# A Griffin-style decoder layer on one core: the first 256 tokens of the gated head outputs are turned to channels by transposing transfers through device memory

## The chip, the cores and the metric

The kernel runs on one core of one Trainium2 chip. The time is device microseconds (us) of that core from launch to end; three runs of the kernel before gave a median of 817.22 us (816.57 to 817.22). The profile is one further execution of the same program.

Engines are named as in the profile: PE is TensorE's matmuls and PEld its weight loads, DVE is VectorE, ACT is ScalarE, POOL is GpSimd, SP is SyncE. "SPq" and "POOLq" are transfers issued by those two. Each engine runs its own instructions in the order in which they stand; engines wait for each other by semaphores.

## The reference

One layer on x of 512 tokens by 1024 channels, in float32. The part that the change touches is branch B, gated linear attention with four heads of 256 output channels:

```python
u = _rmsnorm(h, norm1_g[l])
proj = u @ w_in[l]
a_glu, q, k, v, r, g_low, gate_a, gate_b = _split_cols(proj)
...
o = _gla_chunked(qh, kh, vh, gkh)
o = o * lax.rsqrt(jnp.mean(o * o, axis=-1, keepdims=True) + EPS) * gla_norm_g[l].astype(jnp.float32)
o = o.reshape(bsz, seq, GLA_VDIM).astype(x.dtype) * jax.nn.silu(r)
y_gla = o @ w_gla_out[l]

merged = jax.nn.sigmoid(gate_a) * y_conv + jax.nn.sigmoid(gate_b) * y_gla
h = h + merged @ w_o[l]
```

Behind it stand a second RMSNorm, an up-projection to 2 x 2816 channels with a short convolution, a gated down-projection and a last RMSNorm.

## The kernel before, in words

**Products.** Every float32 operand of a large product is split into a high part `hi` (type float32r, made by an ACT copy) and a low part `lo` (the rest, made by a DVE subtraction), and a product is three matmuls, low by high, high by low and high by high (`mm3`, L537, whose matmuls stand on L541 to L543). Weights come from device memory into four `raw` buffers of 128x1024 words, are split into `whi` (L426, L456) and `wlo` (L427, L464), and are used by TensorE. `weight` (L482) keeps the split weights two steps ahead of their use, and `refill` keeps SP's loads a few tiles ahead of that. The loads stand in SP's order as the list `order` has them (L244 to L274).

**The r-gate.** The projection of r (`seven("w_r", ...)`, L573) is a product of 2x2 blocks in seven steps, a11, a12, s1, n2, s4, n3 and a22. It gives r with tokens on the partitions, in tiles `rt[t, n]` of 128 tokens by 512 channels (t = 0 to 3, n = 0 or 1). `put_r` (L1544) takes each finished tile out of PSUM, applies silu, and multiplies the head outputs `ot[t, n]` by it on DVE (L1561, L1565). The tiles are finished in this order: (0,0) and (1,0) by step a12, (0,1) and (1,1) by s4, (2,1) and (3,1) by n3, (2,0) and (3,0) by a22.

**Turning to channels.** The projection `w_gla` needs the gated outputs with channels on the partitions. `gated_o` (L1246) does that for one 128-channel tile m: four TensorE transposes of 128x128 (one for each 128 tokens) into a PSUM bank `ax` (L1250), an ACT activation that scales by the norm's gain into `hi` (L1257), and a DVE operation that leaves `lo` (L1258). m = 0 to 3 come from n = 0, m = 4 to 7 from n = 1. The eight tiles are called in four pairs: 4 and 5 by `r_at` (L1568) at the end of the r projection, then 6 and 7, 0 and 1, 2 and 3 behind the steps x1, x3 and x2 of the next unit (L1592).

**The unit that follows.** `two_tiles` (L1344) makes two output tiles of a gate projection together, again in seven half-wide steps, in four parts named x1, x3, x2 and x4 after their weights. The first such unit is for `w_gb`, tiles 6 and 7. Its weights are the two loaded tiles (x1, x2) and sums of them made by POOL in `two_sums` (L395, additions on L398). In part x3 ACT copies the accumulators out of PSUM (`put`, L1350, the copy on L1351), and part x2 goes on accumulating in the same banks. Then come `w_gla` 0 and 1, which read all eight turned tiles (`tile_of`, L1444), and the next units.

**Order.** A scheduler in the recording layer orders each engine's instructions. `tc.issue_after(x)` lets what is recorded inside it come only behind the instruction x on its engine. Tiles come from pools with a fixed number of buffers per tag; the tag `btmp` has two, of which one holds the square sums' operand until L1060 and L1061 have read it.

## Time and profile before

| What | Value |
|---|---|
| median of 3 runs | 817.22 us (816.57 to 817.22) |
| the profiled execution, its own time | 816.96 us |
| its span, first to last instruction | 815.3 us |
| granted TensorE clock | 0.998 |
| PE busy in the span | 807.5 us (99%) |
| DVE, ACT, POOL busy | 86%, 60%, 24% |
| TensorE transposes of L1250 | 32, the first at 284.2 us, the last at 296.2 us |

A row of the timeline gives the start in us from the span's start, the duration in us, the engine, the line, the operation, the tile written and those read, the shape, how many such instructions follow one another, and in brackets how long the engine had been idle and what ended it. Durations of matmuls overlap, since they are pipelined: the distance between two starts is what one costs. A row of the DMA issues gives the tile and tensor, the issuing queue, the count, the size of one and the median time from its issue to its landing.

### The profile page before, as it was taken

How to read it: one execution, taken by the hardware profiler on the slowest of the kernel's cores; microseconds unless marked ns; L12 is line 12 of the kernel's file. 1: busy time of each engine (PE TensorE's matmuls, PEld its weight loads, DVE VectorE, ACT ScalarE, POOL GpSimd, SP SyncE). 2: the span in 40 equal slices, each digit the busy share in tenths (PEclk: the TensorE clock that was granted, in tenths of full speed). 3: DMA queues.
4: the chain of work that ended last, by engine and by line, in shares of the span. 5: the costliest groups of instructions: out<-in, count | busy, mean ns of one | idle time of the engine just before them, and what ended most of it. 6: DMA issues, size and time to landing. Idle time of an engine off the chain costs nothing.

```text
span 815.3 us, 11441 instructions
## 1 busy us (share of the span) xinstructions
PE 807.5 (99%) x4215; PEld 693.2 (85%) x4215; DVE 700.7 (86%) x1108; ACT 487.9 (60%) x746; POOL 192.5 (24%) x166
## 2 busy tenths in 40 slices
PE   9999999999999999999999999999999999999996
PEld 7888888788888898989888898898889988899885
DVE  6679999998998988486779899979976999789896
ACT  6667788677546575494435655556435663466655
POOL 2025433332204332122001100320133300522010
PEclk9999999999999999999999999999999999999999
DMA  8487858745831232432458613145732345334662
GB/s 337 146 198 179 187 160 176 161 119 135 186 95 60 78 130 78 137 105 95 164 124 220 190 57 126 52 154 156 144 127 92 142 117 167 105 104 171 165 129 105
DMA packets 36616, 113.60 MB, mean 139 GB/s; under 512 B 3704, under 2 KB 8960, under 8 KB 36560
## 3 DMA queue, kind: packets, MB, share of 16 engines
q1 hardware_dynamic: 29200, 86.92, 30.8%
q0 software_dynamic: 7200, 25.69, 18.0%
q8 instruction: 33, 0.54, 0.3%
q14 instruction: 23, 0.19, 0.1%
q10 hardware_dynamic: 160, 0.27, 0.1%
HBM read 110.76 MB, written 2.10 MB: 138 GB/s over the span
## 4 chain that ended last, share of the span: by engine, by line
PE 84%; DVE 13%; issue 1%; ACT 1%; DMA 1%; SPq 0%; DVEq 0%; ACTq 0%
PE mm L541 20%; PE mm L542 20%; PE mm L543 20%; DVE c L902 5%; PE cv L541 4%; PE cv L542 4%; PE cv L543 4%; DVE aside L902 3%; PE ax L542 2%; PE ax L541 2%; PE ax L543 2%; PE ax L1230 1%; PE ax L1232 1%; DMA kept<-in_w_r_dram 1%; PE ax L1212 0%
## 5 line engine op out<-in xcount | busy, mean ns | idle before, releaser
L541 PE MATMUL mm<-uh,wlo 128*128 128x512 f32 (+1 forms) x532 | 193.9, 364 | 0.2 <-DVE wlo L464 0.2
L542 PE MATMUL mm<-ul,whi 128*128 128x512 f32 (+1 forms) x532 | 191.6, 360 | 0.0
L543 PE MATMUL mm<-uh,whi 128*128 128x512 f32 (+1 forms) x532 | 191.4, 360 | 0.0
L427 DVE TENSOR_TENSOR wlo<-raw,whi 128x1024 fp32r<-128x1024 f32 x82 | 96.0, 1178 | 36.0 <-ACT whi L426 32.2
L398 POOL TENSOR_TENSOR raw<-raw,raw 128x512 f32<-128x512 f32 x39 | 63.9, 1638 | 236.3 <-DVE wlo L427 130.9
L541 PEld LDWEIGHTS mm<-uh,wlo 128*128 128x128 f32 x532 | 100.5, 189 | 15.6 <-DVE wlo L464 0.6
L543 PEld LDWEIGHTS mm<-uh,whi 128*128 128x128 f32 x532 | 100.4, 189 | 15.4
L542 PEld LDWEIGHTS mm<-ul,whi 128*128 128x128 f32 x532 | 100.5, 189 | 14.7
L426 ACT CAST whi<-raw 128x1024 fp32r<-128x1024 f32 x82 | 78.9, 965 | 41.4 <-PE mm L543 24.4
L456 ACT CAST whi<-raw 128x1024 fp32r<-128x1024 f32 x80 | 83.5, 1048 | 27.5 <-PE mm L543 13.9
L464 DVE TENSOR_TENSOR wlo<-raw,whi 128x1024 fp32r<-128x1024 f32 x50 | 66.3, 1331 | 7.1 <-ACT whi L456 6.8
L426 ACT CAST whi<-kept 128x1024 fp32r<-128x1024 f32 (+1 forms) x40 | 40.1, 1008 | 32.4 <-DVE kept L374 16.5
L902 DVE SCALAR_TENSOR_TENSOR aside<-cv,pp,aside 128x255 f32<-128x255 f32 (+6 forms) x112 | 52.2, 466 | 0.0
L902 DVE SCALAR_TENSOR_TENSOR c<-aside,btmp,c 128x247 f32<-128x247 f32 (+13 forms) x93 | 52.1, 565 | 0.0
L427 DVE TENSOR_TENSOR wlo<-kept,whi 128x1024 fp32r<-128x1024 f32 (+1 forms) x40 | 47.5, 1191 | 4.9 <-ACT whi L426 4.7
L902 DVE SCALAR_TENSOR_TENSOR c<-cv,pp,c 128x247 f32<-128x247 f32 (+13 forms) x93 | 43.2, 465 | 1.4 <-ACT c L898 1.4
L458 ACT ACTIVATE wlo<-raw 128x1024 fp32r<-128x1024 f32 x28 | 29.4, 1059 | 19.1 <-PE mm L541 19.1
L1351 ACT COPY tmp<-mm 128x256 f32<-128x256 f32 x38 | 14.1, 370 | 35.1 <-PE mm L543 34.3
L1733 DVE SCALAR_TENSOR_TENSOR tmp<-mm,pp,tmp 128x511 f32<-128x511 f32 (+1 forms) x42 | 31.2, 743 | 3.5 <-ACT tmp L1730 3.4
L1733 DVE SCALAR_TENSOR_TENSOR tmp<-tmp,pp,tmp 128x511 f32<-128x511 f32 (+1 forms) x32 | 27.8, 888 | 0.3
L1504 DVE TENSOR_TENSOR hres<-hres,mm 128x512 f32<-128x512 f32 (+1 forms) x37 | 24.7, 676 | 2.2 <-PE mm L543 2.1
L542 PE MATMUL cv<-ul,whi 128*128 128x512 f32 (+1 forms) x72 | 25.6, 356 | 0.0
(514 smaller groups left out, 2078.3 us busy)
## 6 DMA issues: line engine op xcount, KB each, us to landing
raw<-in_w_up_dram SPq DMA_DIRECT2D x44, 512.0 KB, 3.2
raw<-in_w_glu_dram SPq DMA_DIRECT2D x16, 512.0 KB, 5.1
raw<-in_w_down_dram SPq DMA_DIRECT2D x16, 512.0 KB, 3.4
wlo<-in_w_glu_dram POOLq DMA_DIRECT2D x12, 512.0 KB, 7.1
kept<-in_w_down_dram POOLq DMA_DIRECT2D x9, 512.0 KB, 5.5
raw<-in_w_v_dram SPq DMA_DIRECT2D x8, 512.0 KB, 6.0
raw<-in_w_qk_dram SPq DMA_DIRECT2D x8, 512.0 KB, 6.3
raw<-in_w_gb_dram SPq DMA_DIRECT2D x8, 512.0 KB, 4.0
```

What stands on the lines that cost most here:

```text
L398: work = nc.gpsimd.tensor_tensor(out, x, y, ALU.add)
L426: nc.scalar.copy(hi, raw)
L427: two_low[:] = [nc.vector.tensor_tensor(lo, raw, hi.bitcast(F32), ALU.subtract)]
L456: nc.scalar.copy(hi, raw)
L458: pace[0] = nc.scalar.mul(lo, raw, -1.0)
L464: pace[0] = nc.vector.tensor_tensor(lo, raw, hi.bitcast(F32), ALU.subtract)
L541: nc.tensor.matmul(acc, ll, rh, start=first, stop=False, **kw)
L542: nc.tensor.matmul(acc, lh, rl, start=False, stop=False, **kw)
L543: nc.tensor.matmul(acc, lh, rh, start=False, stop=last, **kw)
L902: nc.vector.scalar_tensor_tensor(out[:, j:], x[:, : half_t - j], w, out[:, j:], ALU.mult, ALU.add)
L1504: done = nc.vector.tensor_tensor(hres[t, n][:, c], hres[t, n][:, c], acc[:, c], op)
L1733: nc.vector.scalar_tensor_tensor(z[:, s:], acc[:, : T - s], w[j], z[:, s:], ALU.mult, ALU.add)
```

## The change

For the first 256 tokens (t = 0 and 1) the turn from tokens to channels leaves TensorE. When `ot[t, n]` is gated (`gate_o`), an ACT copy takes its float32 values apart into their lower and upper 16 bit words, in a tile `planes` of 128 x 2 x 512 words in the tag `btmp`. A transfer issued by POOL writes the tile into a new device memory tensor `words`, one for each n, so that its rows are token and word and its columns channels. When both t are there, `turn_o` issues from SP four transfers with `transpose=True`, each of 512 rows by 128 columns of 16 bit words. One lands as 128 channels by 256 tokens, where the two words of a value lie side by side again. So there are four copies, four writes of 256 KB and eight transposing transfers of 128 KB.

`gated_two` replaces `gated_o`, for two tiles m at once: eight TensorE transposes instead of sixteen, into one bank instead of two, for the tokens from 256 on. `half_o` scales and splits the halves apart, in operations of 256 columns instead of 512: from `turned` for the first half, from PSUM for the second. The first halves of m = 4 to 7 (n = 1) are done behind those of m = 0 to 3. The `hi` copies of the `w_gb` weights that come next are put behind the last `planes` copy on ACT.

```diff
@@ split_weight, the weights in pairs and sevens
-                nc.scalar.copy(hi, raw)
+                with tc.issue_after(behind_planes[0].ins) if behind_planes and spec[0] == "w_gb" else ExitStack():
+                    nc.scalar.copy(hi, raw)
...
-    def gated_o(m, bank):
+    last_silu = []
+    turned, words_of = {}, [dram.tile([T, DV * 2], U16, name=nm("words")) for _ in range(2)]
+
+    def words(t, n):
+
+        planes = tp.tile([P, 2, T], U16, tag="btmp", name=nm("planes"), bufs=2)
+        behind_planes[:] = [nc.scalar.copy(planes, ot[t, n].bitcast(U16).rearrange("p (c two) -> p two c", two=2))]
+        rows = words_of[n][2 * t * P : 2 * (t + 1) * P, :]
+        nc.gpsimd.dma_start(rows.rearrange("(p two) c -> p two c", two=2), planes)
+
+    def turn_o(n):
+        if n == 0:
+            four = rp_.tile([P, 4, H], F32, tag="rx", name=nm("turned"), bufs=1)
+            landing = [four[:, j, :] for j in range(4)]
+        else:
+            twos = [rp_.tile([P, 2, H], F32, tag="r", name=nm("turned"), bufs=6) for _ in range(2)]
+            landing = [two[:, j, :] for two in twos for j in range(2)]
+        for j in range(4):
+            nc.sync.dma_start(landing[j].bitcast(U16), words_of[n][:, j * P : (j + 1) * P], transpose=True)
+            turned[4 * n + j] = landing[j]
+
+    def gated_two(m, bank):
         po = bank()
-        c = (m % 4) * P
-        for p in range(NT):
-            nc.tensor.transpose(po[:, p * P : (p + 1) * P], ot[p, m // 4][:, c : c + P], ident)
-        gain = pp[:, PP_GG + m % 2 : PP_GG + m % 2 + 1]
+        for j in range(2):
+            c = (m % 4 + j) * P
+            for p in (2, 3):
+                at = j * H + (p - 2) * P
+                nc.tensor.transpose(po[:, at : at + P], ot[p, m // 4][:, c : c + P], ident)
+        for j in range(2):
+            start_o(m + j)
+            if m < 4:
+                half_o(m + j, slice(0, H), turned[m + j], last_silu)
+            half_o(m + j, slice(H, T), po[:, j * H : (j + 1) * H], last_silu)
+        if m < 4:
+            for j in range(2):
+                half_o(m + 4 + j, slice(0, H), turned[m + 4 + j], low_at)
...
-        nc.scalar.activation(hi, po, AF.Copy, scale=gain)
-        low_at[:] = [nc.vector.scalar_tensor_tensor(lo, po, gain, hi.bitcast(F32), ALU.mult, ALU.subtract)]
-        oa[m] = hi, lo
+        oa[m] = (both[:, 0, :], both[:, 1, :]) if m < 4 else (heap(F32R), heap(F32R))
+
+    def half_o(m, c, x, behind_op):
+        (hi, lo), gain = oa[m], pp[:, PP_GG + m % 2 : PP_GG + m % 2 + 1]
+        with tc.issue_after(behind_op[0].ins):
+            nc.scalar.activation(hi[:, c], x, AF.Copy, scale=gain)
+            low = nc.vector.scalar_tensor_tensor(lo[:, c], x, gain, hi[:, c].bitcast(F32), ALU.mult, ALU.subtract)
+        if m < 4:
+            low_at[:] = [low]
...
+    def gate_o(t, n):
+        nc.vector.tensor_tensor(ot[t, n], ot[t, n], rt[t, n], ALU.mult)
+        if t < 2:
+            words(t, n)
+        if t == 1:
+            turn_o(n)
...
         if (step, t, n) == ("a22", 3, 0):
-            i, j = gated.pop()
-            nc.vector.tensor_tensor(ot[i, j], ot[i, j], rt[i, j], ALU.mult)
+            gate_o(*gated.pop())
+            gated_two(4, ax_bank)
```

Three places of the built order follow; the rows have line, operation, tile written, tiles read and shape, with the buffer's number in the name.

ACT, from the last weights of the r projection (`kept`) to the first activation of the turned tiles, before. `whi_452`, `whi_455`, `whi_470` and `whi_479` are the w_gb unit's weights for x1, x3, x2 and x4:

```order
L426 CAST whi_450_2649<-kept_349_2138 128x1024
L1555 ACTIVATE r_441_2599<-r_441_2599 128x512
L1555 ACTIVATE r_432_2545<-r_432_2545 128x512
L426 CAST whi_452_2683<-raw_448_2644 128x1024
L426 CAST whi_455_2691<-raw_454_2687 128x1024
L1555 ACTIVATE r_433_2559<-r_433_2559 128x512
L1550 ACTIVATE r_457_2708<-cv_403_2412 128x512
```

The same place on ACT in the changed kernel, where `whi_461` is the weight for x1:

```order
L1255 COPY planes_449_2631<-h_254_1608 128x1024
L429 CAST whi_456_2667<-kept_351_2142 128x1024
L1602 ACTIVATE r_444_2606<-r_444_2606 128x512
L1255 COPY planes_451_2654<-h_345_2129 128x1024
L1602 ACTIVATE r_435_2552<-r_435_2552 128x512
L1602 ACTIVATE r_436_2566<-r_436_2566 128x512
L1255 COPY planes_458_2686<-h_346_2131 128x1024
L429 CAST whi_461_2710<-raw_454_2662 128x1024
L429 CAST whi_464_2718<-raw_463_2714 128x1024
L429 CAST whi_478_2772<-raw_455_2663 128x1024
L1597 ACTIVATE r_466_2735<-cv_405_2416 128x512
```

The last three of the four `planes` copies stand in these rows, all ahead of the unit's first weight; the silu of the last gate (`r_466`) moved behind the weights for x3 and x2.

POOL, the additions for the w_gb unit (`raw_454` is the sum tile) and for the next unit, before:

```order
L398 TENSOR_TENSOR raw_454_2687<-raw_448_2644,raw_449_2645 128x512
L398 TENSOR_TENSOR raw_454_2687<-raw_454_2687,raw_449_2645 128x512
L398 TENSOR_TENSOR raw_449_2645<-raw_449_2645 128x512
L398 TENSOR_TENSOR raw_454_2687<-raw_454_2687,raw_448_2644 128x512
L398 TENSOR_TENSOR raw_501_2929<-raw_488_2852,raw_489_2853 128x512
```

The same place on POOL in the changed kernel, where the sum tile is `raw_463`:

```order
L1257 DMA words_197_1285<-planes_430_2521 128x1024
L400 TENSOR_TENSOR raw_463_2714<-raw_454_2662,raw_455_2663 128x512
L400 TENSOR_TENSOR raw_463_2714<-raw_463_2714,raw_455_2663 128x512
L400 TENSOR_TENSOR raw_455_2663<-raw_455_2663 128x512
L1257 DMA words_197_1285<-planes_449_2631 128x1024
L1257 DMA words_198_1286<-planes_451_2654 128x1024
L1257 DMA words_198_1286<-planes_458_2686 128x1024
L400 TENSOR_TENSOR raw_463_2714<-raw_463_2714,raw_454_2662 128x512
```

One write stands ahead of the additions, and three between the third and the fourth of them.

SP, its loads from the w_gb unit's weights on, before:

```order
L292 DMA raw_448_2644<-in_w_gb_dram 128x1024
L292 DMA raw_449_2645<-in_w_gb_dram 128x1024
L296 DMA raw_472_2754<-in_w_gla_dram 128x1024
L296 DMA raw_481_2804<-in_w_gla_dram 128x1024
L292 DMA raw_488_2852<-in_w_ga_dram 128x1024
L292 DMA raw_489_2853<-in_w_ga_dram 128x1024
```

The same place on SP in the changed kernel:

```order
L294 DMA raw_454_2662<-in_w_gb_dram 128x1024
L294 DMA raw_455_2663<-in_w_gb_dram 128x1024
L298 DMA raw_480_2776<-in_w_gla_dram 128x1024
L1267 DMA_TRANSPOSE turned_450_2634<-words_197_1285 128x512 x4
L1267 DMA_TRANSPOSE turned_459_2689<-words_198_1286 128x512 x2
L1267 DMA_TRANSPOSE turned_460_2690<-words_198_1286 128x512 x2
L298 DMA raw_488_2821<-in_w_gla_dram 128x1024
L294 DMA raw_494_2872<-in_w_ga_dram 128x1024
```

All eight transposing transfers stand between the loads of `w_gla` 0 and `w_gla` 1.

More of the change, by code (lines that the diff above doesn't have):

```diff
@@ L1549, in put_r @@
             rt[t, n] = rp_.tile([P, T], F32, tag="r", name=nm("r"), bufs=6)
-            nc.scalar.activation(rt[t, n], acc, AF.Silu)
+            last_silu[:] = [nc.scalar.activation(rt[t, n], acc, AF.Silu)]
         else:
@@ L1592, in pair_7 @@
             if n == 0 and j < 3:
-                for m in ((6, 7), (0, 1), (2, 3))[j]:
-                    gated_o(m, ax_bank)
+                gated_two((6, 0, 2)[j], ax_bank)
                 if j == 2:
```

15 lines of the change are left out of this document (6 added, 9 removed).

## The prediction

> **What bounds the kernel now.** I read the page's busy times and chain first, then a table by stage around the changed work, then the timelines of each engine there.
>
> ```profile
> PE 807.5 (99%) x4215; PEld 693.2 (85%) x4215; DVE 700.7 (86%) x1108; ACT 487.9 (60%) x746; POOL 192.5 (24%) x166
> PE 84%; DVE 13%; issue 1%; ACT 1%; DMA 1%; SPq 0%; DVEq 0%; ACTq 0%
> core 0: us, PE busy (x) PEld busy (x) DVE busy (x) ACT busy (x) POOL busy (x), PEclk, DMA share, GB/s
> 250.00:284.00 34.00, 33.88 (x150) 27.76 (x149) 31.93 (x30) 21.74 (x28) 11.02 (x7) 1.00 0.18 62
> 284.00:300.00 16.00, 16.00 (x129) 15.49 (x128) 13.29 (x18) 12.73 (x21) 3.44 (x3) 1.00 0.41 133
> ```
>
> TensorE is busy for 99% of the span, and in the 16 us in which the turned tiles are made it never stops, at a full granted clock. So each instruction taken off TensorE there is time won, each wait put in front of it is time lost, and nothing later has room to give either back. DMA has room (busy 0.41), ACT and DVE have 3.3 and 2.7 us of it.
>
> **What is removed.** The PE timeline, with the four pairs of turned tiles:
>
> ```profile
> 284.17 1.03 PE L1250 MATMUL ax<-ident,h 128*128 128x128 f32 x8
> 284.96 0.36 PE L541 MATMUL mm<-uh,wlo 128*128 128x256 f32 x1
> ...
> 287.92 1.04 PE L1250 MATMUL ax<-ident,h 128*128 128x128 f32 x8
> 288.71 0.36 PE L541 MATMUL mm<-hq,wlo 128*128 128x256 f32 x1
> ...
> 291.66 1.04 PE L1250 MATMUL ax<-ident,h 128*128 128x128 f32 x8
> 292.45 0.36 PE L541 MATMUL mm<-sumsq,wlo 128*128 128x256 f32 x1
> ...
> 297.70 0.40 PE L541 MATMUL mm<-oa,wlo 128*128 128x512 f32 x1
> 297.93 0.40 PE L542 MATMUL mm<-oa,whi 128*128 128x512 f32 x1
> ```
>
> Eight transposes cost 284.96 - 284.17 = 0.79 us, 0.099 each. The change drops four of every eight, four times: 4 x 0.395 = 1.58 us. That is the whole gain on the path. It is 0.19% of 817.22, and about 0.2% is what a measurement of this kernel can tell from no change, so even the full gain would just fail to show.
>
> **What is added, off the path if all goes well.** ACT did eight activations of 512 columns and now does sixteen of 256, DVE likewise:
>
> ```profile
> L1257 ACT ACTIVATE h<-ax,pp x4: 677/684/702, 284.9 to 289.7; 128x512 fp32r<-128x512 f32 x4
> L1258 DVE SCALAR_TENSOR_TENSOR h<-ax,pp,h x4: 740/742/746, 286.5 to 291.0; 128x512 fp32r<-128x512 f32 x4
> L1351 ACT COPY tmp<-mm 128x256 f32<-128x256 f32 x38 | 14.1, 370 | 35.1 <-PE mm L543 34.3
> L902 DVE SCALAR_TENSOR_TENSOR c<-cv,pp,c 128x247 f32<-128x247 f32 (+13 forms) x93 | 43.2, 465 | 1.4 <-ACT c L898 1.4
> ```
>
> The rows named `oa` are as many and as long. On ACT 8 x 0.68 = 5.5 us become 16 x 0.37 = 5.9; on DVE 8 x 0.74 = 5.9 become 16 x 0.465 = 7.4. Both increases, 0.4 and 1.5 us, fit in the free time of that stage, if nothing stalls the two queues. Were that cover gone, they would cost those 1.9 us.
>
> The four `planes` copies move 1024 words per partition on ACT. No such copy is in the trace. Nearest are the 1024-column casts, 1.05 us; a copy by 512 columns (0.37 for 256, so about 0.6) is the low end, two of those casts the high end. I take 1.05. The first copy stands behind the gate of `ot[0,0]`, long before anything is short. The last two matter, because of what they wait for.
>
> **The chain that the change puts in front of TensorE.** In the changed order all four copies use one `btmp` buffer (the other is held until the row at 299.53 below has read it), so each must wait until the write of the one before has landed. And the first weights of the w_gb unit stand behind the fourth copy on ACT. What releases each step, from the timelines:
>
> ```profile
> 273.91 2.28 POOL L398 TENSOR_TENSOR raw<-raw 128x512 f32<-128x512 f32 x1
> 282.63 2.26 POOL L398 TENSOR_TENSOR raw<-raw,raw 128x512 f32<-128x512 f32 x1 [6.44 <-DVE wlo L427]
> ...
> 271.00 1.81 DVE L1561 TENSOR_TENSOR h<-h,r 128x512 f32<-128x512 f32 x1
> 275.57 1.18 DVE L1561 TENSOR_TENSOR h<-h,r 128x512 f32<-128x512 f32 x1
> 280.20 2.35 DVE L427 TENSOR_TENSOR wlo<-raw,whi 128x1024 fp32r<-128x1024 f32 x2
> 284.23 1.76 DVE L427 TENSOR_TENSOR wlo<-raw,whi 128x1024 fp32r<-128x1024 f32 x1 [0.47 <-ACT whi L426]
> 299.53 0.68 DVE L1061 TENSOR_TENSOR sum<-btmp,sum 128x512 fp32r<-128x512 f32 x1
> ...
> 271.80 1.05 ACT L426 CAST whi<-kept 128x1024 fp32r<-128x1024 f32 x1
> 283.14 1.05 ACT L426 CAST whi<-raw 128x1024 fp32r<-128x1024 f32 x1 [0.89 <-PE mm L543]
> ```
>
> The gates of the second and third tile are done at 272.81 and 276.75, so the second copy ends at about 273.9. Its write waits on POOL behind three additions of the w_gb unit, which end at 273.91 + 2.28 = 276.19. From there: second write L, third copy 1.05, third write L, fourth copy 1.05, the cast of the x1 weight 1.05, its low part 1.2 (half of 2.35), and six hand-offs of 0.04 (a cast ends at 284.19, its low part begins at 284.23). So x1 can begin at 276.19 + 4.35 + 0.25 + 2L = 280.8 + 2L. TensorE wants it at 284.17 + 0.40 = 284.57. The stall is 2L - 3.8 us, none below L = 1.9. Now this weight is ready at 280.20 + 1.2, with 3.6 us to spare; the change spends that and more.
>
> L is a write of 256 KB to device memory issued by POOL, which the trace does not have. Nearest rows:
>
> ```profile
> out_dram<-hres SPq DMA_DIRECT2D x2, 256.0 KB, 2.0
> out_dram<-y SPq DMA_DIRECT2D x1, 512.0 KB, 2.6
> raw<-in_w_down_dram SPq DMA_DIRECT2D x2, 256.0 KB, 3.0
> raw<-in_w_down_dram POOLq DMA_DIRECT2D x1, 256.0 KB, 3.8
> ```
>
> The same size written by SP lands in 2.0, which is the low end. A POOL transfer of that size that adds to its destination takes 3.8, against 3.0 for a plain load by SP: the high end, since it also reads what it adds to. I take 2.6, the SP write and most of that difference of 0.8. So the stall is 1.4 us, with ends of 0.2 and 3.8, and the net -1.58 + 1.4 = -0.2 (-1.4 to +2.2). Silu of r and the gates of the tiles (2,1) and (3,1) also slip behind the third copy, to about 281.7; the transposes that read them come at 284.17, so that is hidden.
>
> Behind the waiting copies on ACT stand the x3 and x2 weights and the last silus. They end by about 287.5, and x3 is wanted at 286.0 + 2.96 + 0.40 = 289.4, where 2.96 is x1 (284.96 to 287.92) and 0.40 half a group of transposes. On POOL the fourth addition moves from 282.63 to about 287. Its sum is the x4 weight, wanted half a part, 1.5 us, ahead of 297.70; its cast stands on ACT ahead of what x2 waits for and is done by about 290.
>
> **The transposing transfers.** The fourth write lands at 276.19 + 3 x 2.6 + 2 x 1.05 + 0.2 = 286.3. Then come the transfers of n = 1. On ACT the activations that read the first two stand ahead of the copy that empties the accumulator of x3, and part x2 writes that accumulator again. TensorE wants x2 at 289.4 + 2.95 + 0.40 = 292.7 (x3 takes 288.71 to 291.66), so the second of these transfers must land by about 291.4, 5.1 us after its data. Of a 128 KB transposing transfer no row tells; the low end is the 2.0 of the store above, the high end eight of them in sequence at the 2.6 of the 512 KB store each, as if each started when the last had landed. I take the low end to 3 us, with the issue of one hiding the flight of another, as SP's loads do:
>
> ```profile
> 270.49 14.76 SPq L296 DMA_DIRECT2D raw<-in_w_gla_dram  x2
> 286.01 2.19 SPq L292 DMA_DIRECT2D raw<-in_w_ga_dram  x2
> raw<-in_w_gla_dram SPq DMA_DIRECT2D x8, 512.0 KB, 3.7
> ```
>
> Then nothing waits. SP's order holds `w_gla` 1, issued at 270.49 + 14.76 - 0.33 = 284.9, and the two w_ga tiles from 286.01 behind all eight: issued by about 292 instead, they land by 296 to 297, and `w_gla` 1 is read 24 matmuls of 0.23 behind 297.70, at 303.2. That slack covers it, if SP is free by then.
>
> The sum: 816.96 (the profiled execution's own time) - 1.58 + 1.4 = 816.8. The median stands 0.26 above that execution, so **817.0**.
>
> **Where the skill speaks against it.** The TensorE transposes here cost 99 ns each in a row of eight, on 32 bit words. The Trainium skill, VectorE: DVE Perf Modes, section "The three transpose paths", gives 390 ns for TensorE and 1309 ns for the transfer path for a 128x128 bf16 block, and advises TensorE where PSUM can take the result. By it a transfer of four blocks would take an estimated 5.2 us, and the second one of n = 1 would land some 19 us late: about 836. No row here shows such a transfer. What it warns of is rival B, which is priced from rows below.
>
> **The rivals.**
>
> A, the forecast: the writes delay the first weight by about what the transposes save. 817.0, own range 815.6 to 819.5. For it: ACT's order and the single buffer. Against: L is unseen.
>
> B, slower: the transposing transfers run one behind the other, and SP and ACT wait for them. At 2.6 us each, from 278.8 (the second write), the four of n = 0 end at 289.2 and the second of n = 1 at 294.4. ACT's copy for x2 then ends at 295.0 against 292.7, 2.3 us. SP issues `w_gla` 1 at about 297 and it lands at 300.7; its cast stands on ACT ahead of two turned halves, 1.5 us more, and the w_ga weight behind it about 1. Together 4.8 on top of 817.0: 821.8. It decides from (291.4 - 278.8) / 6 = 2.1 us each. For it: eight issues in a row on one queue, next to nothing else to hide in. Against: plain transfers overlap.
>
> C, the full gain: L is near 2.0 and the unit's weight is not late, -1.4 to -1.6: 815.7. For it: the store row, on an almost empty DMA. Against: POOL's transfers are slower than SP's in every row shown.
>
> D, that it does not take the transposes off TensorE, is excluded by the built order: 16 of 32 are left.
>
> **How the numbers follow.** A 0.49, B 0.29, C 0.22. Faster by over 0.2% is below 815.6: half of C, 0.11. Slower by over 0.2% is above 818.9: B without a weak form (0.27) and A's upper end (0.09), 0.36. Within: 0.53. The range has to hold most of B, whose price rises by several us with each further us per transfer: 815.5 to 823, leaving out transfers of 5 us each at one end, and the full gain with something on top at the other.
>
> **What would show it.** Right: 16 transposes left, a PE gap of 1 to 2 us behind the first group of them (x1 waiting for DVE `wlo`), ACT idle before the third and fourth `planes` for the words' landing, writes landing in 2.3 to 3.0. Rival B: a PE gap before x2, with ACT idle before an activation that reads `turned`, and SP's `w_gla` 1 issued after 295. Rival C: no new PE gap over 0.3. I am wrong altogether if `planes` takes 2 us, or if the write's landing is nowhere waited for.

## The result: 1.27 us slower

| | median | fastest to slowest | runs |
|---|---|---|---|
| before | 817.38 us | 816.57 to 818.79 | 20 |
| changed | 818.65 us | 817.94 to 819.39 | 20 |

The ratio is 1.0016, with a 95% interval of 1.0009 to 1.0023. That is under the 0.2% that the prediction set as the bound for a change that can be told in a few runs, but with twenty runs on each side it is clear of no change. The forecast of 817.0 was on the wrong side.

The timeline of PE in the changed kernel, the rows with a gap and two of the groups of transposes in the stretch that the change touches (line numbers are higher by 3 from L427 of before on; L1276 is the transposes):

```profile
279.06 0.47 PE L544 MATMUL cv<-whi,ul 128*128 128x512 f32 x1 [0.29 <-DVE r L1601]
284.62 0.60 PE L1276 MATMUL ax<-ident,h 128*128 128x128 f32 x4
286.97 0.39 PE L544 MATMUL mm<-uh,wlo 128*128 128x256 f32 x1 [1.76 <-DVE wlo L430]
289.95 0.60 PE L1276 MATMUL ax<-ident,h 128*128 128x128 f32 x4
290.31 0.36 PE L544 MATMUL mm<-hq,wlo 128*128 128x256 f32 x1
301.66 0.50 PE L545 MATMUL mm<-oa,whi 128*128 128x512 f32 x1 [0.23 <-DVE oa L1297]
```

Four transposes take 290.31 - 289.95 = 0.36 us, where eight took 0.79: each group saves 0.43. But x1 waits 1.76 us and more for its weight, as forecast, and a second wait stands later, which was not forecast: at the fourth of `w_gla` 0's eight pieces, on the low part of the turned tile 3. DVE made that low part in the second of these rows, behind the low part of a weight:

```profile
300.00 1.22 DVE L467 TENSOR_TENSOR wlo<-raw,whi 128x1024 fp32r<-128x1024 f32 x1
301.13 0.48 DVE L1297 SCALAR_TENSOR_TENSOR oa<-ax,pp,oa 128x256 fp32r<-128x256 f32 x1
```

The rows of the kernel before at the same places, of PE and then of DVE:

```profile
278.62 0.47 PE L541 MATMUL cv<-whi,ul 128*128 128x512 f32 x1
296.19 0.36 PE L541 MATMUL mm<-uh,wlo 128*128 128x256 f32 x1
300.00 0.39 PE L542 MATMUL mm<-oa,whi 128*128 128x512 f32 x1
```

```profile
298.21 1.41 DVE L1258 SCALAR_TENSOR_TENSOR oa<-ax,pp,oa 128x512 fp32r<-128x512 f32 x2
```

In the kernel before, DVE ends that low part at 298.21 + 1.41 = 299.62, and TensorE reads it at 300.00: no wait, but only 0.38 us of room. To compare executions without the chance of how they start, the table counts each from its own first `cv` matmul (278.62 before, 279.06 after), ahead of everything that moves. The last four columns are runs that are told below.

| us from that matmul to | before | changed | own buffers, ACT writes | the same, late weights | only removed | only removed, late weights |
|---|---|---|---|---|---|---|
| first matmul of x1 | 6.34 | 7.91 | 5.93 | 5.88 | 5.89 | 5.92 |
| of x3 | 10.09 | 11.25 | 9.70 | 9.65 | 9.20 | 9.22 |
| of x2 | 13.83 | 14.81 | 13.02 | 12.98 | 12.52 | 12.53 |
| of x4 | 17.57 | 18.28 | 16.33 | 16.29 | 15.83 | 15.84 |
| of `w_gla` 0 | 19.08 | 19.80 | 17.85 | 17.81 | 17.35 | 17.36 |
| product with tile 3's low part | 21.38 | 22.60 | 22.12 | 20.11 | 21.53 | 19.66 |
| that row against before | | +1.22 | +0.74 | -1.27 | +0.15 | -1.72 |
| median against before | | +1.27 | +0.61 | -1.52 | +0.01 | -1.68 |

In the columns "own buffers" and "only removed" the built order has one product of the next tile ahead of the sixth row, 0.23 us that is not lost. Less these 0.23 us, that row gives each result within 0.3 us: what happens by then is nearly the whole difference. In the changed kernel the four groups save 4 x 0.43 = 1.72; x1 costs 7.91 - 6.34 + 0.43 = 2.00, two short waits around x2 0.42, and the low part 22.60 - 19.80 - 2.30 = 0.50, where 2.30 is the distance in the kernel before. 2.92 - 1.72 = 1.20.

The chain that makes x1's weight late, in the changed kernel: POOL, then ACT, DVE and SP.

```profile
271.41 4.12 POOL L400 TENSOR_TENSOR raw<-raw,raw 128x512 f32<-128x512 f32 x2 [9.43 <-DVE r L1601]
275.49 1.74 POOL L400 TENSOR_TENSOR raw<-raw 128x512 f32<-128x512 f32 x1
277.17 0.56 POOL L1257 DMA_DIRECT2D words<-planes  x1
280.99 0.54 POOL L1257 DMA_DIRECT2D words<-planes  x1 [3.25 <-ACT planes L1255]
```

```profile
279.58 1.05 ACT L1255 COPY planes<-h 128x1024 uint16<-128x1024 uint16 x1 [3.94 <-DVE h L1585]
283.67 1.05 ACT L1255 COPY planes<-h 128x1024 uint16<-128x1024 uint16 x1 [1.99 <-DMA words<-planes]
284.62 2.94 ACT L429 CAST whi<-raw 128x1024 fp32r<-128x1024 f32 x3
```

```profile
274.89 1.19 DVE L1585 TENSOR_TENSOR h<-h,r 128x512 f32<-128x512 f32 x1
285.69 3.50 DVE L430 TENSOR_TENSOR wlo<-raw,whi 128x1024 fp32r<-128x1024 f32 x3 [3.21 <-ACT whi L429]
```

```profile
279.53 12.97 SPq L1267 DMA_TRANSPOSE turned<-words  x8
```

The third copy begins at 279.58, and the profile puts its wait down to a gate on DVE. That tile's gate is the row at 274.89, done at 276.08; what came at 279.58 was the landing of the second write, issued at 277.17, 2.41 us before, and SP's first transfer, which needs the same landing, begins at 279.53. It is a wait for several semaphores, of which the row names the wrong one.

### The profile page after: what moved, and what is told of

The parts are those of the page before. It is cut to its first block, busy times and chain, and to the rows that moved or that the text cites. A ratio compares the mean times of both kernels' runs of the same rounds, so it can differ in the third digit from the quotient of the medians.

```text
span 816.9 us, 11451 instructions
## 1 busy us (share of the span) xinstructions
PE 807.5 (99%) x4199; PEld 691.8 (85%) x4199; DVE 704.4 (86%) x1116; ACT 492.3 (60%) x758; POOL 192.7 (24%) x170
## 4 chain that ended last, share of the span: by engine, by line
PE 85%; DVE 12%; ACT 1%; issue 1%; DMA 0%; DVEq 0%; ACTq 0%
PE mm L544 19%; PE mm L545 19%; PE mm L546 19%; DVE c L905 5%; PE cv L544 4%; PE cv L545 4%; PE cv L546 4%; DVE aside L905 3%; PE ax L545 2%; PE ax L546 2%; PE ax L544 2%; PE mm L761 2%; PE ax L1233 1%; PE cv L761 1%; DVE wlo L430 1%
## 5 line engine op out<-in xcount | busy, mean ns | idle before, releaser
L400 POOL TENSOR_TENSOR raw<-raw,raw 128x512 f32<-128x512 f32 x39 | 62.1, 1592 | 229.3 <-DVE wlo L430 116.5
```

The lines of the kernel that those rows point to most:

```text
L400: work = nc.gpsimd.tensor_tensor(out, x, y, ALU.add)
```

## Experiment 1: take the x1 chain apart

Four runs, made together (the kernel before: 817.50 us). The first gives each copy a buffer of its own, the second moves the issue of the writes:

```diff
-        planes = tp.tile([P, 2, T], U16, tag="btmp", name=nm("planes"), bufs=2)
+        planes = hp.tile([P, 2, T], U16, tag="h", name=nm("planes"))
```

> The changed kernel, but each `planes` copy takes a buffer of its own, so that no copy waits for the write before it to land; everything else stays. Theory 1 (TensorE lost 1.95 us at the first matmul of x1, because the weight stood on ACT behind a copy that waited for the landing of the third write): that wait falls to under 0.3 us, the PE gap before x1 is gone, and the time falls by 1.5 to 2 us against the changed kernel, to 0.3 to 0.6 us below the kernel before - unless ACT, whose order the new buffers also move (the halves that read the n = 1 transfers now stand ahead of the copies that empty the accumulator of x3), waits for the first of these transfers at about 288.7: then a new gap of 1.5 to 2 us before x3 takes its place and the time is as the changed kernel's. Theory 2 (the added cost is in the 256 column operations on ACT and DVE, not in the writes): the gap before x1 may shrink, but the end still comes as late as now, 1.2 us above the kernel before, without any new gap before x3.

```diff
-        nc.gpsimd.dma_start(rows.rearrange("(p two) c -> p two c", two=2), planes)
+        nc.scalar.dma_start(rows.rearrange("(p two) c -> p two c", two=2), planes)
```

> The changed kernel, but the writes of the words are issued from ACT, right behind each copy, instead of from POOL, where the second one stands behind three additions. The copies still share one buffer and still wait for each other's landing. Theory 1 (the chain through POOL makes x1's weight late): the second write leaves about 2 us earlier (275.1 instead of 277.2), each further round is shorter by the 0.5 us of an issue from POOL and the 0.4 us hand-off, so x1's weight is ready before 284.6 and the PE gap of 1.76 us before x1 falls under 0.3 us; time 0.5 to 1.1 us below the kernel before. Theory 2 (256 column operations): no change against the changed kernel beyond 0.3 us. A third outcome: an issue from ACT holds that engine as long as POOL's did, and the gap only halves; then about 0.2 us above the kernel before.

Own buffers: 822.77 us, 5.27 above the kernel before, ratio 1.0062 (1.0049 to 1.0074). The gap before x1 is gone, and two others are there (PE, then ACT):

```profile
290.58 0.38 PE L544 MATMUL mm<-hq,wlo 128*128 128x256 f32 x1 [1.50 <-ACT tmp L1391]
305.21 0.50 PE L545 MATMUL mm<-oa,whi 128*128 128x512 f32 x1 [2.61 <-DVE oa L1297]
```

```profile
288.00 0.51 ACT L1296 ACTIVATE h<-turned,pp 128x256 fp32r<-128x256 f32 x1 [2.79 <-DMA turned<-words]
```

The one before x3 was expected as a possibility: ACT stands 2.79 us for a transposing transfer of n = 1, ahead of the copy that frees the accumulator. That outcome had the time equal to the changed kernel's, though, and it is 4 us longer. The wait of 2.61 us in `w_gla` was not expected, and theory 1 does not explain it. In that trace DVE makes the low parts of two later weights, 2.28 us each, at 300.28 and 302.48, between the last halves of tiles 2 and 3: it is the wait that experiments 2 and 3 take up. The two gaps together do not make up the 5.27 us; where the rest is lost stays open.

Writes from ACT: 817.35 us, ratio 1.0000 (0.9991 to 1.0009). The chain was not what had been expected. The second write does leave early, at 274.13, but ACT's new order puts the third copy behind a silu that waits for DVE, so it begins at 279.53 as before, and x1 still waits 1.53 us. That it is 1.3 us better than the changed kernel comes in part from the built order, which put three products that belong later, 0.23 us each, into the wait on tile 3's low part; the wait in front of x2 is gone too.

The other two runs take the two sides of the change apart. The first keeps all copies, writes and transfers, but inside `gated_two` each tile is made as by the old `gated_o`, and `turned` is unread. The second does only what is removed:

```diff
 def gated_two(m, bank):
-    po = bank()
...
     for j in range(2):
         start_o(m + j)
+        po = bank()
+        c = ((m + j) % 4) * P
+        for p in range(NT):
+            nc.tensor.transpose(po[:, p * P : (p + 1) * P], ot[p, m // 4][:, c : c + P], ident)
```

```diff
 def gate_o(t, n):
-        if t < 2:
-            words(t, n)
         if t == 1:
-            turn_o(n)
+            for j in range(4):
+                turned[4 * n + j] = ot[j // 2, n][:, (j % 2) * H : (j % 2 + 1) * H]
```

> Only what the change adds ahead of the transposes: the copies, the writes and the transposing transfers are all issued as in the changed kernel, but nobody reads `turned`; TensorE makes all 32 transposes and ACT and DVE work by 512 columns, as in the kernel before. The transfers are thus work that the result does not need. Theory 1: the gap before x1 is there in full (1.8 to 2.0 us) and nothing pays for it: 1.8 to 2.2 us above the kernel before, and no waits in the first part of w_gla. Theory 2 (the halves are the cost): within 0.4 us of the kernel before.

> Only what the change removes and the halves it needs: no copies into words, no writes, no transposing transfers. The first half of each turned tile is read straight from the gated tile, so the first 256 tokens stay unturned: that turning is left out of the computation. 16 transposes are gone from TensorE, ACT and DVE work by 256 columns as in the changed kernel. Theory 1: no gap before x1, and the 1.58 us of the transposes are gained, less what the halves cost in the first part of w_gla: if the 0.6 us of short waits there come from the halves alone, 0.9 to 1.1 us below the kernel before; if they come from the lateness of the transfers, 1.5 to 1.6 us below. Theory 2 (the halves are the main cost): no more than 0.3 us below the kernel before.

Added alone: 821.89 us, 4.39 above, twice what was expected. The rows of PE:

```profile
287.10 0.39 PE L544 MATMUL mm<-uh,wlo 128*128 128x256 f32 x1 [1.32 <-DVE wlo L430]
295.06 0.66 PE L1275 MATMUL ax<-ident,h 128*128 128x128 f32 x4 [0.65 <-DVE h L1279]
299.55 0.66 PE L1275 MATMUL ax<-ident,h 128*128 128x128 f32 x4 [0.53 <-DVE oa L1279]
300.54 0.39 PE L544 MATMUL mm<-uh,wlo 128*128 128x256 f32 x1 [0.33 <-DVE tmp L1389]
```

The late weights also made DVE late, and with two PSUM banks per group, as before the change, the next transposes wait until DVE has read the banks. In the changed kernel, with one bank per group, these waits are not there. So the change's two sides don't add up (4.39 and, below, 0.01 against 1.27 for both): its smaller groups hide part of what its writes cost.

Removed alone: 817.51 us against 817.50, ratio 1.0001 (0.9992 to 1.0010). This was the run that turned the study. With no copy, write or transfer at all, 16 transposes fewer gain nothing: at the start of `w_gla` 0 TensorE is 1.73 us ahead, and at tile 3's low part it is 0.15 behind. DVE there:

```profile
297.26 0.48 DVE L1297 SCALAR_TENSOR_TENSOR oa<-ax,pp,oa 128x256 fp32r<-128x256 f32 x1
297.66 2.29 DVE L430 TENSOR_TENSOR wlo<-raw,whi 128x1024 fp32r<-128x1024 f32 x1
299.87 0.47 DVE L1297 SCALAR_TENSOR_TENSOR oa<-ax,pp,oa 128x256 fp32r<-128x256 f32 x1
```

Between the last half of tile 2 and that of tile 3 DVE makes the low part of a `w_ga` weight, which TensorE wants only behind all of `w_gla` 0. Tile 3's low part ends at 300.34, which is 21.48 us after the first `cv` matmul (278.86 in this trace), against 21.00 in the kernel before. The weight's low part took 2.29 us instead of 1.22, beside an addition on POOL: that alone is 1.07 of the 1.36 us for which TensorE stands idle.

## Experiment 2: what the low parts wait for

From this came theory 3: what TensorE gains ahead of `w_gla` 0 can't come through, because DVE ends the last low parts no earlier; only 0.38 us of room stands there. Four runs (before: 817.51 us) tried it from several sides. One drops the rule on the casts, one changes only the order of the groups in the kernel before, one does that with the removal alone, one both with the complete change:

```diff
-                with tc.issue_after(behind_planes[0].ins) if behind_planes and spec[0] == "w_gb" else ExitStack():
+                with ExitStack():
                     nc.scalar.copy(hi, raw)
```

```diff
-                gated_two((6, 0, 2)[j], ax_bank)
+                gated_two((0, 2, 6)[j], ax_bank)
```

> The changed kernel without the rule that puts the casts of the w_gb weights behind the last `planes` copy on ACT: now the casts for x1 and x3 stand ahead of the fourth copy. Nothing else is edited. Theory 1 (x1 waits because its cast stands behind the copy that waits for a landing): the gap of 1.76 us before x1 is gone, and x4 begins about 1 us earlier than in the kernel before. Theory 3 (formed from the run that only removed: TensorE reaches the first product of w_gla that needs the last low part of tile 3 with 0.38 us to spare in the kernel before, and DVE does not finish that part earlier when TensorE is earlier): what is won by then is waited off at that product, in one wait of 1 to 1.5 us on the low part of `oa`; time 817.2 to 817.8, as the kernel before. Theory 1 alone, without 3: 816.2 to 816.6.

> The kernel before with one thing of the order changed: the three groups of turned tiles in the w_gb unit are (0, 1), (2, 3), (6, 7) instead of (6, 7), (0, 1), (2, 3), so that the tiles made last are those that w_gla reads last (the seventh and eighth eighth of its products instead of the third and fourth). Same work. Theory 3: no wait stands there now, only 0.38 us of room, so the time stays within 0.3 us of the kernel before. If the order by itself is worth something, it is faster by 0.5 us or more.

> Only the removal (no copies, writes or transposing transfers; the first half of each turned tile is read straight from the gated tile, so the first 256 tokens stay unturned and that turning is left out of the computation), and the order (0, 1), (2, 3), (6, 7) of the groups. Theory 3: the low parts made last are wanted about 2 us later than in the run that only removed, the wait of 1.4 us on them is gone and the 1.58 us of the 16 transposes come through: 1.2 to 1.6 us below the kernel before. If the halves cost by their number on DVE whatever is wanted when: no more than 0.4 us below, with the wait at another product.

> The changed kernel, complete, with two edits: the casts of the w_gb weights are not put behind the `planes` copies, and the groups come in the order (0, 1), (2, 3), (6, 7). Theories 1 and 3 together: no gap before x1, and the low parts that are made last are wanted 2 us later; 0.8 to 1.5 us below the kernel before, unless the activations that read the transfers of n = 1 wait for their landing, which would show as ACT idle before one of them and a gap before x2 or x3. If only theory 1 is right: 0.8 to 1.2 us below as well, but then the run with free casts alone has it too. If neither: as the changed kernel, 1.2 us above.

The order in the kernel before: 817.43 us, no change, as expected. The other three missed. Free casts: 819.76 us, 2.25 above. The gap before x1 is gone, but ACT and DVE carry the same work in another order, and waits of another kind add up (the waits of PE, with the total in us, how many, and the longest; then ACT):

```profile
PE mm L544 <- ACT tmp L1391: 1.2, 2, 0.9
PE mm L544 <- ACT oa L1296: 0.8, 1, 0.8
PE mm L545 <- DVE oa L1297: 0.7, 1, 0.7
```

```profile
300.11 1.05 ACT L459 CAST whi<-raw 128x1024 fp32r<-128x1024 f32 x1 [0.84 <-DMA raw<-in_w_gla_dram]
```

ACT stood for the load of a later `w_gla` weight, issued on SP behind the transposing transfers, with the last half of a turned tile queued behind that cast.

The removal with the other order: 817.32 us, ratio 0.9999 (0.9990 to 1.0007), not the 1.2 to 1.6 expected. The tiles made last are now wanted 2 us later, and DVE made them later too, so that TensorE still waits for one (0.59 us idle at 302.39; the rest of the missing gain is in no wait that this stretch of the trace shows):

```profile
297.96 1.74 DVE L1064 TENSOR_TENSOR sum<-btmp,sum 128x512 fp32r<-128x512 f32 x1
299.62 2.32 DVE L430 TENSOR_TENSOR wlo<-raw,whi 128x1024 fp32r<-128x1024 f32 x1
301.86 0.47 DVE L1300 SCALAR_TENSOR_TENSOR h<-ax,pp,h 128x256 fp32r<-128x256 f32 x1
```

So moving the moment at which the low part is wanted was not enough; what DVE does ahead of it came next. Both edits in the complete kernel: 818.09 us, 0.58 above, with waits, in a traced execution that was itself 1.3 us above the median, of 1.3 us for late gates in front of transposes, and 0.6 on a low part.

## Experiment 3: the order on DVE

Theory 3 was then put more sharply: the low parts of later weights must stand behind the last halves on DVE. The edit notes the low part of the last half and puts the later ones behind it. The casts of these weights are put into the same rule, but `last_half` is an instruction of DVE. On ACT the built order moved by one cast: the one that stood ahead of tile 3's last activation stands behind it, in the complete kernel (297.43 without the edit, the activation at 298.61; with it 297.94 and 297.56) and in the removal alone.

```diff
+    def later():
+        return tc.issue_after(last_half[0].ins) if last_half else ExitStack()
...
-                with tc.issue_after(behind_planes[0].ins) if behind_planes and spec[0] == "w_gb" else ExitStack():
+                with tc.issue_after(behind_planes[0].ins) if behind_planes and spec[0] == "w_gb" else later():
                     nc.scalar.copy(hi, raw)
-                two_low[:] = [nc.vector.tensor_tensor(lo, raw, hi.bitcast(F32), ALU.subtract)]
+                with later():
+                    two_low[:] = [nc.vector.tensor_tensor(lo, raw, hi.bitcast(F32), ALU.subtract)]
...
-            nc.scalar.copy(hi, raw)
+            with later():
+                nc.scalar.copy(hi, raw)
...
-                pace[0] = nc.vector.tensor_tensor(lo, raw, hi.bitcast(F32), ALU.subtract)
+                with later():
+                    pace[0] = nc.vector.tensor_tensor(lo, raw, hi.bitcast(F32), ALU.subtract)
...
                 if j == 2:
+                    last_half[:] = newest
                     start_norms()
```

Four runs (before: 817.48 us): the halved transposes without halves, the removal with this edit, the complete change with own buffers and writes from ACT (the two edits of experiment 1 together), and that with this edit. The first, against the kernel before:

```diff
-        for p in range(NT):
-            nc.tensor.transpose(po[:, p * P : (p + 1) * P], ot[p, m // 4][:, c : c + P], ident)
+        for p in (0, 1):
+            nc.tensor.transpose(po[:, p * P : (p + 1) * P], ot[p + 2, m // 4][:, c : c + P], ident)
+        po = po[:, : 2 * P].unsqueeze(1).to_broadcast([P, 2, 2 * P])
```

> The kernel before with 16 of its 32 transposes, and nothing split: each activation of 512 columns and each low part of 512 columns stays one instruction and reads the 256 columns of the last two token tiles twice. So the first 256 tokens get the values of the last 256: their turning is left out of the computation. No writes, no transfers, no halves. Theory 3a (the halves, 8 more instructions each on ACT and DVE, are what keeps the 1.58 us from coming through): 1.2 to 1.6 us below the kernel before. Theory 3b (in w_gla's first products TensorE is held by DVE's queue, whatever the width of the pieces): 0.3 to 0.5 us below, the room of 0.38 us that stands there now, with a wait of about 1.1 us on a low part of `oa`.

> Only the removal, in halves (no writes or transfers; the first half of each turned tile is read straight from the gated tile, so the first 256 tokens stay unturned, and that turning is left out), and one change of order: the low parts of the weights that come later (w_gla 1, the first of w_ga) stand behind the last halves on DVE, where they stood between them. Theory 3 (the last halves are late because DVE makes later weights first, at 1.2 us each and 2.3 us beside additions on POOL): no wait on a low part of `oa` or `h` over 0.3 us, 1.2 to 1.6 us below the kernel before. If the halves are late for another reason (their activations on ACT): within 0.4 us of the kernel before, the wait stays.

> The changed kernel, complete, with each `planes` copy in a buffer of its own and the writes issued from ACT. Theory 1: no landing is waited for by a copy, and none is late: no gap over 0.3 us before x1, and the transfers of n = 1 start about 2 us earlier than with own buffers alone, so that the gap of 1.5 us before x3 is gone too. Theory 3: what is won is waited off in w_gla's first products, 0.3 us above to 0.5 us below the kernel before. Without theory 3: 1.2 to 1.6 us below.

> The same complete kernel (own buffers, writes from ACT), and the low parts of later weights behind the last halves on DVE. Theories 1 and 3 together: no wait in front of x1, x3 or w_gla's first products over 0.3 us, 1.0 to 1.6 us below the kernel before, the whole gain of the 16 transposes. If the transfers cost by something else (the load of w_gla 1 behind them on SP, traffic): it shows as a wait of w_gla's second tile, and the time is 0.5 to 1 us worse than that.

| run | median | against before | ratio |
|---|---|---|---|
| 16 transposes, no halves | 815.90 us | -1.58 | 0.9979 (0.9971 to 0.9988) |
| only removed, late weights | 815.80 us | -1.68 | 0.9982 (0.9973 to 0.9991) |
| complete, own buffers, ACT writes | 818.09 us | +0.61 | 1.0007 (0.9999 to 1.0016) |
| the same, late weights | 815.96 us | -1.52 | 0.9982 (0.9973 to 0.9991) |

Without halves the whole 1.58 comes through, with the weights' low parts still ahead of the last low parts on DVE: they end at 299.14 there, 19.71 us after the first `cv` matmul against 21.00 in the kernel before, with TensorE 1.5 us early. So of theory 3 the part "whatever the width" fell: DVE follows TensorE if its work stays as it was. What holds it up is the halves, 16 low parts in the place of 8, placed between later weights. With these weights behind them the halves cost nothing either. The complete kernel without and with the edit, on DVE:

```profile
296.96 1.22 DVE L467 TENSOR_TENSOR wlo<-raw,whi 128x1024 fp32r<-128x1024 f32 x1
298.09 0.48 DVE L1297 SCALAR_TENSOR_TENSOR oa<-ax,pp,oa 128x256 fp32r<-128x256 f32 x1
298.48 2.29 DVE L430 TENSOR_TENSOR wlo<-raw,whi 128x1024 fp32r<-128x1024 f32 x1
300.70 0.47 DVE L1297 SCALAR_TENSOR_TENSOR oa<-ax,pp,oa 128x256 fp32r<-128x256 f32 x1
```

```profile
297.05 0.48 DVE L1303 SCALAR_TENSOR_TENSOR oa<-ax,pp,oa 128x256 fp32r<-128x256 f32 x1 [0.22 <-ACT oa L1302]
298.07 0.48 DVE L1303 SCALAR_TENSOR_TENSOR oa<-ax,pp,oa 128x256 fp32r<-128x256 f32 x1 [0.54 <-ACT oa L1302]
299.26 1.22 DVE L473 TENSOR_TENSOR wlo<-raw,whi 128x1024 fp32r<-128x1024 f32 x1
```

Without the edit tile 3's low part ends at 301.17 and the product waits 1.36 us for it; with it, at 298.55, and DVE is waiting for ACT, not TensorE for DVE. The cast that moved on ACT has a part in this, and no run has the one without the other. Had it stayed, tile 3's activation would have ended at 299.08, as it did without the edit, and its low part 0.52 later, 20.49 us after the first `cv` matmul against the 20.11 at which TensorE takes it now. That makes an estimate of at most 0.4 us of the 2.13 between the two kernels; the rest goes with the order on DVE. The complete kernel without the edit was expected at most 0.3 above the kernel before, so its 0.61 is a miss by 0.3. The complete kernel with the edit, with all its copies, writes and transfers, is within 0.16 us of the removal that has none: in this order they cost next to nothing, and a cost of the transfers by their traffic, the rival that was left, is not seen. The last of these kernels computes all that the reference asks and beats both the kernel before and the changed one.

## Experiment 4: how the loss divides

Each of two kernels (before: 817.39 us) has the order edit alone, one on the changed kernel, one on the kernel before.

> The changed kernel with the order edit alone: the low parts of w_gla 1 and of the first w_ga weights stand behind the last halves on DVE; buffers and writes stay as in the changed kernel. Theory 1 and 3 as two terms that add up: the gap of 1.76 us before x1 stays, the waits in w_gla's first products (the start of its products slid by 0.5 to 0.75 us there) go; 0.4 to 0.8 us above the kernel before. If x1's lateness is the whole cost and the later waits only follow from it: no change against the changed kernel, 1.2 us above. If the later waits are the whole of what can be seen: at or below the kernel before.

> The kernel before with the same order edit: the low parts of later weights behind the last of the turned tiles' low parts on DVE. Nothing waits there in the kernel before, so theory 3 expects no change: within 0.3 us. If the order edit is worth something of itself, 0.5 us or more below.

On the kernel before: 817.50 us, ratio 1.0000 (0.9991 to 1.0009): nothing waits there, nothing is gained. On the changed kernel: 818.58 us, 1.19 above, practically the changed kernel's time, and not the 0.4 to 0.8 that two terms which add up would give. On DVE no later weight stands ahead of tile 3's last half now, but that half still comes late, from ACT, where the cast of the `w_ga` weight stands ahead of it (ACT, then DVE):

```profile
299.07 1.07 ACT L432 CAST whi<-raw 128x1024 fp32r<-128x1024 f32 x1
300.01 0.51 ACT L1302 ACTIVATE oa<-ax,pp 128x256 fp32r<-128x256 f32 x1
```

```profile
300.55 0.48 DVE L1303 SCALAR_TENSOR_TENSOR oa<-ax,pp,oa 128x256 fp32r<-128x256 f32 x1 [0.83 <-ACT oa L1302]
```

So the two causes don't divide the 1.27 us into shares. Taking away x1's lateness alone leaves +0.61, the order on DVE alone +1.19, both together -1.52. With x1 late by 2 us, TensorE comes so late to tile 3 that its low part is nearly there; when x1 is on time, the wait there grows from 0.50 to 22.12 - 17.85 - 2.30 - 0.23 = 1.74 us and takes the gain.

## Why the prediction was wrong, by its steps

- **The gain**, forecast 1.58: right. Measured 0.43 a group, 1.72, in the table, and 1.52 to 1.68 in medians wherever nothing waits.
- **The chain before x1**: the mechanism was right (single buffer, ACT's order, two landings). L was taken as 2.6, and the landings took 2.3 to 2.6; the copy was taken as 1.05 and took 1.04. By the Trainium skill, DMA: Bandwidth & Descriptors, section "Anatomy of one DMA — SWDGE (gpsimd) path", a transfer from GpSimd takes about 2.0 us plus its bytes at 436 GB/s, an estimated 2.6 for these 256 KB; the trace agrees. The term that was mis-sized is "three additions of the w_gb unit, which end at 273.91 + 2.28 = 276.19": they ended at 277.23, and 0.44 of this is the offset of the execution. The other 0.6 is not the change's doing. Counted from the first `cv` matmul, the additions end 2.43 us ahead of it in the trace of before and 1.82 or 1.83 ahead in all fifteen others, with those of the kernel before in another order among them. In the trace of before the first addition began 0.03 us ahead of DVE's gate, which took 1.81 us (the row at 271.00), and the second ahead of the low part behind that gate, which took 2.16 (at 272.88). In all others the gate began first and took 0.68 or 0.69, the low part took 1.22 or 1.23, and it was the second addition, begun behind it, that took longer, 2.24 to 2.37 instead of 1.62. The rows of POOL before and of DVE in the changed kernel:

```profile
270.97 1.28 POOL L398 TENSOR_TENSOR raw<-raw,raw 128x512 f32<-128x512 f32 x1 [11.87 <-DMA raw<-in_w_gb_dram]
```

```profile
271.25 0.68 DVE L1585 TENSOR_TENSOR h<-h,r 128x512 f32<-128x512 f32 x1
```

  So the term was read off an execution that was the exception, which one trace could not tell me. From the end of the additions to x1's first matmul 286.97 - 277.23 = 9.74 us passed, where the prediction had 9.80. The "six hand-offs of 0.04" also hold from ACT to DVE only: from ACT's copy to POOL's issue it was 280.99 - 280.63 = 0.36. The stall was 2.0 instead of 1.4, 0.6 of the 1.4 us by which the sum was off.
- **The halves "fit in the free time of that stage, if nothing stalls the two queues"**, and after it **"Then nothing waits"**: this is the step that failed. It put at nothing two waits that measured 0.50 and 0.42, together 0.9 us, and the first of them grows to 1.74 when x1 is on time. I weighed the halves by the free time of DVE in 284 to 300, 2.7 us, and never asked at which moment TensorE needs the last of them. There the room was 0.38 us, with low parts of weights that nobody needs yet in the same queue. The row at 298.21 and that at 300.00 were in the trace of before and would have told of the room, though not that the halves would keep DVE from ending that low part earlier: that took the runs without halves and with the later weights moved. The size of a half was near right on DVE (0.47 to 0.48 against 0.465) and low on ACT (0.46 to 0.54 against 0.37).
- **Rival C**, the full gain if L is near 2.0, had a chance of 0.22, and L was not near 2.0. Nor would that have been enough: with x1 on time and DVE's order as it was, the complete kernel is still 0.61 us slower than before.
- **Rival B** fell: the transposing transfers held SP's queue for 1.12 to 1.26 us each, under the 2.1 from which that rival was to decide, landed 2.6 to 3.6 us after their issue and overlapped, and in the changed kernel no activation waits for one. That they are long in SP's queue did show, when the order brought ACT to them sooner (2.79 us with own buffers).
- The slack that was to cover **x3 and x2** held for x3. Around x2 0.42 us were lost, the larger part because ACT's copy of the accumulator came late. The prediction had the x4 weight's cast, which stands on ACT ahead of what x2 waits for, "done by about 290"; ACT stood 1.20 us for POOL's fourth addition and was done with it at 290.99, a consequence of the same chain:

```profile
290.37 0.62 ACT L429 CAST whi<-raw 128x512 fp32r<-128x512 f32 x1 [1.20 <-POOL raw L400]
```

So the sum would have read -1.72 + 2.0 + 0.42 + 0.50 = +1.20, and the measured change was +1.27. The 0.42 is worked out from the trace; no run takes it away by itself.

## What to carry to other kernels

When TensorE gets faster in one stage, look for the next place where it reads what another engine makes, and read off there how long the operand has been ready: without more, that room is what can be gained, whatever the free time of the engine over the stage. More comes through only if the other engine makes the operand earlier too: with 16 transposes and whole tiles it did (19.71 against 21.00 us), and all 1.58 us came, while in halves between later weights it did not. An engine with 17% of free time still decides if it makes what is wanted last ahead of what is wanted first; here putting the low parts of two later weights behind the last halves, with one cast on ACT, was worth 2.1 of the 2.8 us between the changed kernel and the fastest, once x1 was on time. And of two waits in a row, removing one alone shows little, so try them together before either is called harmless.

## What the runs showed of the hardware

- A subtraction of a weight's low part on DVE takes 1.22 us alone, and an addition on POOL 1.28 to 1.30. Beside an addition that has begun first the subtraction takes up to 2.3 us; beside work of DVE that has begun first it is the addition that takes longer, here 3.81. Rows from the removal alone (POOL), then from the fastest of the complete kernels (POOL and DVE):

```profile
297.56 1.30 POOL L400 TENSOR_TENSOR raw<-raw,raw 128x512 f32<-128x512 f32 x1 [13.02 <-DVE wlo L467]
```

```profile
300.70 3.81 POOL L403 TENSOR_TENSOR raw<-raw,raw 128x512 f32<-128x512 f32 x1 [13.89 <-DVE wlo L473]
304.58 1.28 POOL L403 TENSOR_TENSOR raw<-raw,raw 128x512 f32<-128x512 f32 x1
301.00 1.22 DVE L434 TENSOR_TENSOR wlo<-raw,whi 128x1024 fp32r<-128x1024 f32 x1
```

  The first began 0.10 us ahead of the low part of 2.29 us shown above and took no longer than alone; the second began while DVE was at work, and took 3.81 beside low parts of 1.22; the third, which began when these were done, took 1.28. That fits what the Trainium skill, SBUF — State Buffer, section "SBUF: two separate sides", says of the port pair that the two engines share: whichever has it holds it for a whole instruction, and the other is blocked. So the price changes sides with the order: in this last kernel POOL pays, where nobody waits for it.
- A transposing transfer of 128 KB of 16 bit words holds SP's queue for 1.12 to 1.26 us in the changed kernel and lands 2.6 to 3.6 us after its issue (up to 4.2 in other runs), with several in flight (eight issues and their waits in the 12.97 us above). The 5.2 us each, one behind the other, that the prediction worked out from the Trainium skill, VectorE: DVE Perf Modes, section "The three transpose paths", are not borne out.
- Issuing a write of 256 KB holds POOL for 0.54 to 0.66 us and ACT for 0.34 to 0.39. It lands in 2.3 to 2.6 us from POOL in the changed kernel (once in 3.7, with own buffers) and in 2.0 to 3.4 from ACT.
